# Opening a fused attention and retention layer: the first projection group as a written-out pipeline over the tiles of x

## The chip, the cores and the metric

The kernel runs on one core of one Trainium2 chip. The metric is the device time of one launch in microseconds. Of the kernel before, three timed runs and one profiled execution are at hand. The engines are named as in the profile: PE (TensorE; PEld are its weight loads), ACT (ScalarE), DVE (VectorE), POOL (GpSimd) and SP, which issues the DMAs. SPq is SP's queue.

## The reference

One layer of a streaming encoder works on 2048 prompt rows and 64 sample rows of width 1024. Only its beginning matters here:

```python
def layer_inputs(x, norm_g, w_in, b_gate, qn_g, kn_g):
    h = rmsnorm(x, norm_g) @ w_in
    qa, ka, va, za, qb, kb, vb, zb, ga, gb = jnp.split(h, _split_points(), axis=-1)
    ...

def rmsnorm(x, g=None):
    xf = x.astype(jnp.float32)
    y = xf * lax.rsqrt(jnp.mean(xf * xf, axis=-1, keepdims=True) + EPS)
    if g is not None:
        y = y * g.astype(jnp.float32)
    return y.astype(x.dtype)
```

The rest of the layer is differential attention (prompt rows among themselves, sample rows against a cache of 4096 keys), a retention branch, two gated output projections, a last projection and the residual. The first group of columns computed is va, the 512 columns of the attention's values, which are also an output.

## The kernel before, in words

**Precision.** The big products are made from two parts. A float32 operand a is split into a high part (`h`, a cast) and a low part (`l`, the rest), and a product is the sum of three matmuls: high by high, high by low, low by high. x is kept normalised, transposed and split as `xh` and `xl`; a piece of W (128 rows by 512 columns in the groups that matter here) as `wh` and `wl`.

**Tiles and groups.** x is worked on in two halves of 1024 rows. The first has nine tiles: eight of 128 prompt rows and one of the 64 sample rows. A group is 512 (wide) or 256 columns of W applied to all tiles of the half. The first three groups of the first half are wide: va, then ka, then qa. A tile of a wide group is eight chunks of the inner dimension, three matmuls each, 24 matmuls of 512 columns, into one of two PSUM buffers `mm`.

**From x to xh and xl.** `x_prep` (L250) issues the load of a tile and spawns `x_norm` (L303), which puts on ACT the square with its row sum (L308), a logarithm and an exponential (L310, L311); on DVE the mean (L315), a Newton step for the inverse root (L318 to L320), and the scaling of the tile by the root and the norm row (L327, two halves of 512 in the first half of x). `x_tile` (L331) transposes the scaled tile on PE in two lots of four (L341, into the single PSUM buffers `tp` and `pv`), casts each lot to `xh` on ACT (L348) and subtracts to `xl` on DVE (L349).

**The norm row.** In the first half `norm_g` is loaded as one row into `gz` and spread to 128 partitions by a matmul of one row of a constant matrix `ones` with it (`spread`, L285, L290); the sum stays in the two PSUM buffers `s` and is read by L327. Ten calls of `warm` follow (L297), each a matmul of `ones` by itself that nobody reads. Six such calls stand ahead of everything (L1667).

**W.** `w_load` (L365) issues the pieces of W into staging buffers, the first eight at once, the rest when more than four tiles of x are ready. `w_split` (L405) casts each piece on ACT (L415) and subtracts on POOL (L422), two of the first eight on DVE (L419).

**The first tile.** `mm_first` (L459) does the 16 matmuls with `wh` first (L470) and then the 8 with `wl` (L475); the other tiles go through `mm_group` (L442, L451). After a tile, `fin_va` copies the sums twice on ACT (L600, L602), subtracts on DVE (L604) and stores three times; its buffer `thi` exists once.

**What sets the order.** The program is a set of generators (tasks) run by `loop` (L82) with a planner's clock: `self.pe` is the planned time of PE, and A, V, G and ld advance planned times of ACT, DVE, POOL and the DMAs. A task yields a time or a condition and is resumed when the planned time is reached; among tasks that are ready the smallest priority number goes first. So the order of instructions on PE, ACT and DVE, the three engines named in `MANUAL` (L1676), is the order in which the tasks happen to put them; these engines then work strictly by semaphores. `x_prep`, `w_load` and `w_split` have priority 0, `x_norm` 1, `x_tiles` 2, and the stream of groups (`w_stream`, L1552, calling `natural`, L478) 9. POOL and SP are not in `MANUAL`; their instructions are placed by the framework. Loads are gated by `XFLY` (three tiles of x in flight in the first half) and by the count of W pieces issued: x tile 1 may go after four pieces, tile 2 after eight (L262).

Of the kernel before, what the change touches and what calls it, by code (L numbers as in the profile page):

```python
# [8 lines left out]
F32 = mybir.dt.float32  # L9
# [3 lines left out]
ALU = mybir.AluOpType  # L13
# [3 lines left out]
T = 2048  # L17
NS = 64
TT = T + NS
D = 1024  # L20
KC = 8
PAST = 4096
EPS = 1e-6
# [13 lines left out]
LAT = 250.0  # L37
# [6 lines left out]
STAGE = ["ws", "ws", "ws", "ath", "ath", "atl", "atl", "ev"]  # L44

# [11 lines left out]
class Hybrid:  # L57
# [192 lines left out]
    def x_prep(self, half):  # L250
        nc = self.nc
        self.xq = []
        self.xfly = 0
        yield from self.take("row", 2)
        gn = self.row("gn") if half else None
        jk = self.row("xjk")
        if half == 0:
            self.give("row", 0.0)
        tiles = self.xtiles(half)
        left = [len(tiles)]  # L260
        for j, (src, r, seg, col) in enumerate(tiles):
            yield lambda: self.xfly < XFLY[half] and (half > 0 or self.wloads >= min(4 * j, 8))  # L262
            self.xfly += 1
            yield from self.take("row")
            xt = self.row("xt")[:r]
            self.xq.append(None)
            tx = self.ld(xt, src, 4096 * r)
            if j == 0 and half == 0:
                yield from self.take("row")
                gz = self.row("gz")  # L270
# [3 lines left out]
                tg = t + 1200  # L274
                self.spawn(self.spread(gn, gz, t), 10)
# [9 lines left out]
    def spread(self, gn, gz, t):  # L285

        yield t
        for k in range(2):
            yield from self.take("s")
            self.nc.tensor.matmul(gn[k], self.ones[0:1, :], gz[0:1, 512 * k:512 * k + 512], start=True, stop=True)  # L290
# [12 lines left out]
    def x_norm(self, j, xt, jk, gn, t, tg, r, seg, col, left):  # L303
        nc = self.nc
        yield t
# [3 lines left out]
        t = self.A(1024, self.pe, 190)  # L309
# [3 lines left out]
        t2 = self.A(1, 0, 40)  # L313
        yield t
        nc.vector.tensor_scalar(ms, ss, 1.0 / D, EPS, op0=ALU.mult, op1=ALU.add)  # L315
        self.V(1, t)
        yield t2
        nc.vector.tensor_scalar(ms, y, y, ms, op0=ALU.mult, op1=ALU.mult)  # L318
        nc.vector.tensor_scalar(ms, ms, -0.5, 1.5, op0=ALU.mult, op1=ALU.add)
        nc.vector.tensor_scalar(y, y, ms, 128.0 if isinstance(gn, list) else 1.0, op0=ALU.mult, op1=ALU.mult)  # L320
        for _ in range(3):
            t = self.V(20, t2)
        if tg > self.pe:
            yield tg
        for k, g in enumerate(gn if isinstance(gn, list) else [gn]):
            sl = slice(512 * k, 512 * k + g.shape[1])
            nc.vector.scalar_tensor_tensor(out=xt[:, sl], in0=xt[:, sl], scalar=y, in1=g[:r], op0=ALU.mult, op1=ALU.mult)  # L327
        self.xq[j] = (xt, self.V(1100, t), r, seg, col)
        left[0] -= 1

    def x_tile(self, j):  # L331
# [3 lines left out]
        yield t  # L335
# [69 lines left out]
    def w_split(self):  # L405
        nc = self.nc
        nw = n = 0
        for c0, wide in self.order[0] + self.order[1]:
            for q in range(8 if wide else 4):
                yield lambda: len(self.wst) > 0  # L410
                st, t, tag = self.wst.pop(0)
                (h, l), tags = yield from self.w_room(wide, nw, q)
                if t > self.pe:
                    yield t
                nc.scalar.copy(h, st)  # L415
                th = t = self.A(512, self.pe)
                if n in (4, 6):
                    yield t
                    nc.vector.tensor_sub(l, st, h.bitcast(F32))  # L419
                    t = self.V(512, t)  # L420
                else:
                    nc.gpsimd.tensor_sub(l, st, h.bitcast(F32))  # L422
                    t = self.G(512, t)
                self.give(tag, t)
                if wide:
                    self.wq.append((h, l, t, tags, th))
                else:
                    self.wq.append((h[:, 0], l[:, 0], t, (), th))
                    self.wq.append((h[:, 1], l[:, 1], t, tags, th))
                n += 1  # L430
            nw += wide
# [10 lines left out]
    def mm_group(self, ps, n, us, wsl, x, wfirst, last):  # L442
        nc = self.nc
        seg, xsl = x
        for c in range(KC):
# [10 lines left out]
            if c % 2 and c < KC - 1:  # L456
                yield self.pe

    def mm_first(self, ps, us, r):  # L459

        nc = self.nc
        xh, xl = self.xh[0], self.xl[0]
        for c in range(KC):
            if len(us) <= c:
                yield lambda: len(self.wq) > 0
                us.append(self.wq.pop(0))
            if us[c][4] > self.pe:
                yield us[c][4]
            for i, x in enumerate((xh, xl)):
                nc.tensor.matmul(ps, x[:, c, :r], us[c][0], start=c == 0 and i == 0, stop=False)  # L470
                self.P(512)
        for c in range(KC):
            if us[c][2] > self.pe:
                yield us[c][2]
            nc.tensor.matmul(ps, xh[:, c, :r], us[c][1], start=False, stop=c == KC - 1)  # L475
            self.P(512)

    def natural(self, half, fin, fresh=False, wide=False):  # L478
        us = []
        tiles = self.xtiles(half)  # L480
        per, n = (1, 512) if wide else (2, 256)
        for j0 in range(0, len(tiles), per):
# [3 lines left out]
            for u, (src, r, seg, col) in enumerate(group):  # L486
                if fresh:
                    yield lambda: len(self.xt_ready) > j0 + u
                    yield self.xt_ready[j0 + u]
                if fresh and j0 == 0 and wide:  # L490
                    yield from self.mm_first(ps, us, r)
                else:
                    yield from self.mm_group(ps[:r, n * u:n * u + n], n, us, slice(0, n),
                                             (seg, slice(col, col + r)), False, j0 + u == len(tiles) - 1)
                if u < len(group) - 1:
                    yield self.pe
# [1055 lines left out]
    def w_stream(self):  # L1552
# [28 lines left out]
        self.seg_free = [0.0, 0.0]  # L1581
        self.xh, self.xl = [None, None], [None, None]
        self.wst = []
# [4 lines left out]
        self.spawn(self.x_tiles(9), 2, "w")  # L1588
# [52 lines left out]
    def run(self):  # L1641
# [18 lines left out]
        with tc.manual_schedule(engines=MANUAL(ET)):  # L1660
# [6 lines left out]
            self.warm(6)  # L1667
# [73 lines left out]
```

## Time and profile before

| what | value |
|---|---|
| three timed runs | 2017.9, 2019.16, 2020.87 us; median 2019.16 |
| profiled execution, time | 2016.98 us |
| its span | 2015.2 us |
| mean granted clock of PE | 0.997 |
| PE busy | 1991.4 us, 99% of the span |
| ACT, DVE, POOL busy | 956.9, 992.8, 419.2 us |
| one 512-column matmul in the first group, start to start | 0.23 us |
| ACT's square of a tile of x (L308) | 1.06 us |
| ACT's cast of a piece of W (L415) | 0.62 us |
| POOL's subtraction of a piece of W (L422) | 1.27 to 1.74 us in the first 80 us |
| load of a tile of x, 512 KB, issue to landing | 3.5 to 8.3 us |

The profile is of one execution. A line of a timeline gives the start and the duration in us, the engine, the line of the kernel, the operation, the tile written and the tiles read, shapes and a count; in brackets stands the time that the engine was idle before it and what released it. Matmuls are pipelined, so durations of neighbours overlap, and the distance of starts is the better measure. A line of the table of stages gives, for a stretch of time, the busy time of PE, PEld, DVE, ACT and POOL with the number of instructions, then the granted clock of PE as a share of full speed, the share of time that the DMA engines were busy, and GB/s. Time to landing is from a DMA's issue to its end.

### The profile page before, as it was taken

What the parts mean: (1) busy time and instruction counts of PE and PEld (TensorE: products, weight loads), DVE (VectorE), ACT (ScalarE), POOL (GpSimd) and SP (SyncE); (2) the same over time, 40 slices, a digit from 0 to 9 for tenths busy, and PEclk for the clock granted to TensorE, in tenths of its full rate; (3) what the DMA queues carried; (4) which work ended last, traced back from release to release, by engine and by line L of the source; (5) the groups of instructions that cost most, each with busy time, mean ns of one, the idle gap of its engine ahead of it and who ended that gap; (6) DMA issues with size and microseconds to landing.
All of it is one profiled execution on the core that took longest, in us unless ns stands there. A gap on an engine that the chain in (4) does not pass through costs nothing. (4 is left out here: it accounts for less than half of the span.)

```text
span 2015.2 us, 34341 instructions
## 1 busy us (share of the span) xinstructions
PE 1991.4 (99%) x12414; PEld 1786.1 (89%) x12414; DVE 992.8 (49%) x2659; ACT 956.9 (47%) x2096; POOL 419.2 (21%) x387
## 2 busy tenths in 40 slices
PE   8999999999999999999999999999999989999999
PEld 6778999999998999999999888888888878889997
DVE  6353575553331321546856655635653365444442
ACT  6332676654432433535666665645654544333221
POOL 2310121121112221221211111222112443222210
PEclk9999999999999999999999999999999999999999
DMA  6646464344565463563352252463234665444431
GB/s 228 195 146 171 135 168 130 101 140 144 150 182 131 135 178 104 164 198 123 112 157 87 85 158 68 124 190 95 64 92 126 202 216 159 144 146 133 140 94 58
DMA packets 330268, 280.96 MB, mean 139 GB/s; under 512 B 64689, under 2 KB 296113, under 8 KB 330098
## 3 DMA queue, kind: packets, MB, share of 16 engines
q1 hardware_dynamic: 330098, 278.77, 46.8%
q8 instruction: 98, 1.61, 0.3%
q14 instruction: 72, 0.59, 0.1%
HBM read 187.19 MB, written 91.49 MB: 138 GB/s over the span
## 5 line engine op out<-in xcount | busy, mean ns | idle before, releaser
L451 PE MATMUL mm<-xh,wh 128*128 128x512 f32 (+2 forms) x1280 | 461.1, 360 | 0.0
L451 PE MATMUL mm<-xh,wl 128*128 128x512 f32 (+2 forms) x1280 | 451.7, 353 | 0.0
L451 PE MATMUL mm<-xl,wh 128*128 128x512 f32 (+2 forms) x1280 | 450.9, 352 | 0.0
L422 POOL TENSOR_TENSOR wl<-ws,wh 128x512 fp32r<-128x512 f32 x190 | 251.9, 1338 | 912.3 <-ACT wh L415 632.2
L451 PE MATMUL mm<-wh,xh 128*128 128x256 f32 (+3 forms) x864 | 272.5, 315 | 0.3 <-DVE tlo L604 0.3
L451 PEld LDWEIGHTS mm<-xh,wl 128*128 128x128 f32 x1280 | 240.9, 188 | 31.9
L451 PEld LDWEIGHTS mm<-xh,wh 128*128 128x128 f32 x1280 | 241.2, 188 | 29.6 <-issue 0.2
L451 PEld LDWEIGHTS mm<-xl,wh 128*128 128x128 f32 x1280 | 241.5, 189 | 29.1
L451 PE MATMUL mm<-wh,xl 128*128 128x256 f32 (+3 forms) x864 | 267.2, 309 | 0.0
L451 PE MATMUL mm<-wl,xh 128*128 128x256 f32 (+3 forms) x864 | 266.9, 309 | 0.0
L661 ACT COPY ev<-mm 128x512 f32<-128x512 f32 x140 | 71.6, 511 | 238.8 <-PE mm L451 216.9
L451 PEld LDWEIGHTS mm<-wh,xh 128*128 128x128 f32 (+1 forms) x864 | 162.5, 188 | 11.0 <-PE s L836 0.4
L451 PEld LDWEIGHTS mm<-wl,xh 128*128 128x128 f32 (+1 forms) x864 | 162.7, 188 | 10.6
L451 PEld LDWEIGHTS mm<-wh,xl 128*128 128x128 f32 (+1 forms) x864 | 162.5, 188 | 10.2
L957 DVE TENSOR_TENSOR atl<-at,ath 128x512 fp32r<-128x512 f32 (+1 forms) x144 | 93.8, 660 | 139.8 <-ACT ath L955 139.8
L874 ACT ACTIVATE row<-row,a_mx 128x1024 f32<-128x1024 f32 (+7 forms) x160 | 153.6, 964 | 16.7 <-DVE a_mx L854 16.6
L844 DVE CUSTOM_DVE_ANT_0 row<-s,dfar 128x512 f32<-128x512 f32 (+2 forms) x192 | 117.9, 632 | 74.7 <-PE s L836 73.5
L415 ACT CAST wh<-ws 128x512 fp32r<-128x512 f32 x192 | 117.0, 619 | 40.7 <-PE mm L451 28.3
L955 ACT CAST ath<-at 128x512 fp32r<-128x512 f32 (+1 forms) x144 | 79.6, 563 | 99.3 <-PE at L942 96.9
L835 PE MATMUL s<-K,q 128*128 128x512 f32 (+3 forms) x320 | 120.3, 381 | 2.5 <-DVE a_acc L844 2.5
L836 PE MATMUL s<-K,q 128*128 128x512 f32 (+3 forms) x320 | 115.5, 362 | 0.7 <-DMA q<-qT 0.7
L895 DVE SCALAR_TENSOR_TENSOR row<-row,a_w 128x1024 f32<-128x1024 f32 (+4 forms) x96 | 98.1, 1032 | 26.7 <-ACT row L892 26.5
(206 smaller groups left out, 3945.5 us busy)
## 6 DMA issues: line engine op xcount, KB each, us to landing
ws<-in_w_in_dram SPq DMA_DIRECT2D x192, 256.0 KB, 3.1
q<-qT SPq DMA_DIRECT2D x128, 128.0 KB, 3.0
V<-vN SPq DMA_DIRECT2D x24, 512.0 KB, 5.5
K<-kT SPq DMA_DIRECT2D x48, 256.0 KB, 4.4
gt<-gaT SPq DMA_DIRECT2D x64, 132.0 KB, 2.1
gt<-gbT SPq DMA_DIRECT2D x64, 132.0 KB, 2.2
xt<-in_x_prompt_dram SPq DMA_DIRECT2D x16, 512.0 KB, 6.3
kn<-in_cache_k_T_dram SPq DMA_DIRECT2D x32, 256.0 KB, 3.9
```

The source lines that it names most:

```text
L415: nc.scalar.copy(h, st)
L422: nc.gpsimd.tensor_sub(l, st, h.bitcast(F32))
L451: nc.tensor.matmul(ps, p, q, start=c == 0 and i == 0, stop=c == KC - 1 and i == 2)
L661: nc.scalar.copy(ev, ps)
L835: nc.tensor.matmul(ps, q1s, kk, start=True, stop=False)
L836: nc.tensor.matmul(ps, q2s, kk, start=False, stop=True)
L844: nc.vector.tensor_tensor_reduce(out=units[k0 // 1024][:, k0 % 1024:k0 % 1024 + n], in0=ps, in1=tab, scale=-SLOPES[h], scalar=3.0e38, op0= ...
L874: nc.scalar.activation(u, u, AF.Exp, bias=mx, scale=-1.0, accum_out=lp[:, k:k + 1])
L895: nc.vector.scalar_tensor_tensor(out=u0, in0=u0, scalar=w[:, 0:1], in1=u1, op0=ALU.mult, op1=ALU.add)
L955: nc.scalar.copy(ah[:, :w], at[:, :w])
L957: nc.vector.tensor_sub(al[:, :w], at[:, :w], ah[:, :w].bitcast(F32))
```

## The change

The first group no longer goes through `natural` and four tasks; a new function `opening` writes the order of all its work out. `mm_first` and the task `x_tiles` for the first half are gone; `x_norm` is cut into four functions (`norm_sums` on ACT, `norm_mean`, `norm_root` and `norm_scale` on DVE) that `opening` calls one by one; `w_split` is cut into `w_piece` (cast on ACT) and `w_low` (subtraction), and waits until the opening is over. `between`, called by `mm_group` after the second and the fourth chunk of a tile, puts the sums of tile j+2 and then the transposes of tile j+1 and the scaling of tile j+2 into tile j. In tile 0 the order of the 24 matmuls is a list: H is `xh` by `wh`, X is `xl` by `wh`, L is `xh` by `wl`, T1 the transposes of tile 1.

x tile 1 is loaded ahead of all of W. Of the first eight pieces of W, three are subtracted on DVE (the fifth, seventh and eighth) instead of two. The norm row is put in a `gz` of 128 rows, of which the others are zeroed by a memset on DVE and one on POOL, and is spread by matmuls over all 128 rows; its load comes after that of `ident` instead of before. Ten warm calls stand ahead in place of six, and five after the spread in place of ten.

The core of the diff:

```diff
+OPENING = [(k[0], int(k[1])) for k in ("H0 X0 H1 X1 H2 X2 L0 H3 X3 L1 H4 X4 L2 T1 H5 X5 L3 H6 X6 L4 "
+                                       "H7 X7 L5 L6 L7").split()]
...
     def x_prep(self, half):
...
-            yield lambda: self.xfly < XFLY[half] and (half > 0 or self.wloads >= min(4 * j, 8))
+            yield lambda: self.xfly < XFLY[half] and (half > 0 or j < 2 or self.wloads >= 8)
...
-                t = self.ld(gz[0:1, :], self.i["norm_g"][0:1, :], 4096)
+                self.nc.vector.memset(gz[:, :512], 0.0)
+                self.nc.gpsimd.memset(gz[:, 512:], 0.0)
                 self.ld(self.ident, self.i["c_ident"], 1 << 16)
+                tg = self.ld(gz[0:1, :], self.i["norm_g"][0:1, :], 4096)
...
-            self.spawn(self.x_norm(j, xt, jk, gn, tx, tg, r, seg, col, left), 1, "w")
+            self.xin.append([xt, jk, gn, tx, tg, r, seg, col, left])
+            if half:
+                self.spawn(self.x_norm(j), 1, "w")
...
-            self.nc.tensor.matmul(gn[k], self.ones[0:1, :], gz[0:1, 512 * k:512 * k + 512], start=True, stop=True)
+            self.nc.tensor.matmul(ps, self.ones, gz[:, 512 * k:512 * k + 512], start=True, stop=True)
             t = self.P(2048)
         self.give("row", t)
-        for _ in range(10):
-            yield self.pe
-            self.warm(1)
+        self.warm(5)
...
-                if n in (4, 6):
-                    yield t
-                    nc.vector.tensor_sub(l, st, h.bitcast(F32))
...
+    def w_low(self, wide, n, st, h, l, t, tag, tags):
+        th = t
+        if n in (5, 7, 8):
+            self.nc.vector.tensor_sub(l, st, h.bitcast(F32))
...
             if c % 2 and c < KC - 1:
                 yield self.pe
+                if between:
+                    yield from between(c)
+
+    def opening(self, fin):
...
+        yield lambda: len(self.xin) > 0
+        self.norm_sums(0)
+        self.norm_mean(0)
+        self.norm_root(0)
+        yield from self.spread()
+        self.norm_scale(0)
+        yield lambda: len(self.xin) > 1
+        self.norm_sums(1)
+        for _ in range(2):
+            yield from (yield from self.w_piece(False))
+        self.norm_mean(1)
+        self.norm_root(1)
+        yield from self.x_tile(0, False)
+        self.norm_scale(1)
+        for _ in range(6):
+            low.append((yield from self.w_piece(False)))
+        for g in low[:4]:
+            yield from g
...
+        for k, c in OPENING:
+            if k == "T":
+                yield from self.x_tile(1, False)
+                self.norm_sums(2)
+                for g in low[4:]:
+                    yield from g
...
+                self.norm_mean(2)
+                self.norm_root(2)
+                continue
...
+            nc.tensor.matmul(ps, x, w, start=(k, c) == ("H", 0), stop=(k, c) == ("L", KC - 1))
...
+        self.spawn(fin(ps, 128, 1, 0, self.pe + LAT), 0, "w")
+        self.norm_scale(2)
+        self.opened = True
+        for j in range(1, 9):
+            def between(c):
+                if c == 1 and j + 2 < 9:
+                    yield lambda: len(self.xin) > j + 2
+                    self.norm_sums(j + 2)
+                if c == 3 and j + 1 < 9:
+                    if j + 2 < 9:
+                        self.norm_mean(j + 2)
+                        self.norm_root(j + 2)
+                    yield from self.x_tile(j + 1, False)
+                    if j + 2 < 9:
+                        self.norm_scale(j + 2)
...
+            yield from self.mm_group(ps[:r], 512, us, slice(0, 512), (seg, slice(col, col + r)), False,
+                                     j == 8, between)
...
     def natural(self, half, fin, fresh=False, wide=False):
+        if fresh and wide:
+            yield from self.opening(fin)
+            return
...
-            self.warm(6)
+            self.warm(10)
```

More of the change, by code (lines that the diff above doesn't have):

```diff
@@ L250, in x_prep @@
     def x_prep(self, half):
-        nc = self.nc
         self.xq = []
+        self.xin = []
         self.xfly = 0
[L254 to L258, printed above, removed]
+        gn = jk = tg = None
+        if half:
+            yield from self.take("row", 2)
+            gn, jk = self.row("gn"), self.row("xjk")
+        else:
+            yield from self.take("row")
+            jk = self.row("xjk")
         tiles = self.xtiles(half)
```

163 lines of the change are left out of this document (98 added, 65 removed).

## The prediction

> **What bounds the kernel now.** I read the page first: engine shares and the chain that ended last.
>
> ```profile
> span 2015.2 us, 34341 instructions
> PE 1991.4 (99%) x12414; PEld 1786.1 (89%) x12414; DVE 992.8 (49%) x2659; ACT 956.9 (47%) x2096; POOL 419.2 (21%) x387
> ```
>
> PE is the bound almost everywhere, so the change can only earn what PE loses in the first group. Then the timeline of PE over the first 80 us, to see where it loses time; columns are start, duration, instruction, and in brackets the idle time before it and its releaser.
>
> ```profile
> 1.05 2.93 PE L300 MATMUL at<-ones 128*128 128x128 f32 x12 [1.05 <-DVE epst L1666]
> 4.21 3.78 PE L290 MATMUL s<-gz,ones 1*128 1x512 f32 x4 [0.23 <-DMA gz<-in_norm_g_dram]
> 7.92 4.51 PE L300 MATMUL at<-ones 128*128 128x128 f32 x20
> 12.27 0.60 PE L341 MATMUL tp<-ident,xt 128*128 128x128 f32 x4
> ...
> 13.54 0.49 PE L470 MATMUL mm<-wh,xh 128*128 128x512 f32 x1 [0.24 <-ACT xh L348]
> ...
> 20.97 0.39 PE L451 MATMUL mm<-wh,xh 128*128 128x512 f32 x1
> ...
> 31.36 0.66 PE L341 MATMUL tp<-ident,xt 128*128 128x128 f32 x4 [3.86 <-DVE xl L349]
> ```
>
> The first useful matmul starts at 13.54, tile 1 at 20.97 (the first L451), and PE stands 3.86 us before 31.36. The same view puts the first matmul of the next group at 76.93. Third, the timeline of DVE says why PE stood: the two xl subtractions of x tile 2 start only at 30.63 and 31.23, because the norm scaling of a later tile was queued ahead of them.
>
> ```profile
> 27.77 0.69 DVE L604 TENSOR_TENSOR tlo<-mm,thi 128x512 fp32r<-128x512 f32 x1 [0.23 <-ACT raw L602]
> ...
> 29.30 1.41 DVE L327 SCALAR_TENSOR_TENSOR xt<-xt,x_st,s 128x512 f32<-128x512 f32 x2
> ...
> 30.63 0.68 DVE L349 TENSOR_TENSOR xl<-tp,xh 128x512 fp32r<-128x512 f32 x1
> ```
>
> Fourth, the table of stages (last three columns: granted clock, DMA share, GB/s) shows what the stand cost afterwards.
>
> ```profile
> 31.00:32.00 1.00, 0.64 (x5) 0.46 (x5) 0.91 (x2) 0.00 (x0) 0.00 (x0) 1.00 0.98 351
> 32.00:33.00 1.00, 1.00 (x7) 0.93 (x7) 0.32 (x1) 0.94 (x2) 0.00 (x0) 0.82 0.17 31
> 33.00:34.00 1.00, 1.00 (x4) 0.71 (x3) 0.37 (x1) 0.97 (x3) 0.00 (x0) 0.50 0.15 37
> ```
>
> The clock fell to 0.50 and came back at 36.0; matmuls start 0.43 us apart there and 0.2285 us elsewhere.
>
> **What the stage would be without loss.** A tile is 24 matmuls x 0.2285 = 5.48 us. Its eight transposes add 0.88 (46.84 to 47.63, plus 0.09 on the slower first matmul); the 64-row sample's add 0.7. Tiles 1 to 8 hold 192 matmuls (43.87), the transposes of tiles 2 to 7 (5.28) and of the sample (0.7): 49.85 us. They took 76.93 - 20.97 = 55.96, so 6.1 us are lost: 4.0 of standing, the rest at the half clock.
>
> **The change, part by part.**
>
> *Warm matmuls and spread.* Ten calls in place of six make 20 records; 20 take 4.32 us at 7.92, so they run from 1.05 to 5.4. The grant column says 1.00 here, but these records are 0.216 us apart at 128 columns, so I take the clock to be half; the four transposes of 12.27 (0.43 to the next four, against 0.60 at 31.36) are the first fast ones. The spread keeps its four records. At the old spacing (0.865) they end at 8.9, at a full clock (0.43) at 7.1. The row gz now waits for two memsets. That on VectorE: 128 columns take 0.165 and one takes 0.06, so 512 take some 0.5 and end at 1.6. That on GpSimd is not in the trace: above 0.10 (its 128x1 memset), below 1.27 (its 128x512 subtraction, which does more); I take 0.7, in between. So gz is issued at 1.6 to 2.2 instead of 1.20, and by the old 3.0 us is there at 4.6 to 5.2, still under the warm matmuls: nothing on PE. But x1 and all of W queue behind it on SP, up to 0.6 us; I charge 0.3. Scaled x0 is ready at 8.4 to 9.9 (VectorE is free at 6.85; two scalings of 0.75, the second after the spread), the five warm calls behind the spread end at 8.0 (fast) to 11.2 (slow), so x0 is transposed between 8.4 and 11.2, not 12.13.
>
> [...] The row: full-height matmuls from 7.92 to 12.2 came before the first fast record; one-row ones from 4.21 to 7.9 brought no fast one. [...]
>
> *x1 ahead of W.* Landings in before, as issue plus time to landing: x0 4.2, w0 6.2, w1 8.0, w2 8.8, w3 9.3, x1 10.7, w4 11.3, w7 13.3, x2 14.5. x1 (512 KB) takes the place of w0 and w1, so it lands near 8.0 + 0.3; w0 and w1 near 9.1 and 9.6; w2 to w7 after that up to 13.6, x2 as before. On ACT the new order is: square and root of x1, then casts of w0 and w1, then xh of x0. From a square's start to the cast behind it takes 1.63 (13.86 to 15.49), casts are 0.55 apart: square 8.3, w0 9.93, w1 10.48, xh 11.0, first matmul 11.65 (xh to matmul 0.64, as 12.90 to 13.54). That is **1.9 us earlier**; x0's transposes are hidden. Bounds: x1 at 6.2 (w0's place) gives 9.9, x1 at 10.7 (its own old place) gives 14.0: -3.6 to +0.5.
>
> *Tile 0, written out.* Counted from its first matmul. X0 follows at 0.73 as before. W casts follow the two xh at 1.1, 1.65, 2.2, 2.7, 3.3, 3.85, ahead of H2 to H7. GpSimd subtracts w0 and w1 before and w2, w3, w5 until 5.4 (1.3 each): L0 to L3 and L5 don't wait. The transposes of x1 come at 3.5 (scaled at 2.8). VectorE: two xl until 1.3, scaling of x1 until 2.8, w4's part until 4.1, x1's xl until 6.0, then w6 and w7 at 0.85 each (the smaller of the two such rows, 0.85 and 1.77, GpSimd being idle then): 6.9 and 7.75. So L6 and L7 wait, and the tile ends at 8.05; without a wait it would be 6.4. Before it took 20.97 - 13.54 = 7.43: **0.6 us lost**. Bounds: both parts at 0.69 (the cheapest 512-column subtraction) give 7.7, both at 1.77 give 9.9.
>
> *Tiles 1 to 8.* Per tile of 6.36 us, ACT has two copies, two xh, square and roots: 1.2 + 1.1 + 1.65 = 3.95; VectorE 0.69 + 1.4 + 0.9 + 1.41 = 4.4. In the new order the xl of tile j+1 stand ahead of the scaling of tile j+2. From the tile's start: copies until 1.35, square and roots until 3.1, transposes at 2.75, xl ready at 5.4, needed at 6.36; scaling ends at 6.8, needed at 9.1. The stand of 3.86 goes, and with it the fall of the clock. What is late next is the xl, with 1.0 us to spare, then the W casts of the next group in ACT's queue. I keep 0.5 us of loss: 50.35 against 55.96, **5.6 us saved**. Bounds: 6.1 saved, or with 0.5 us of loss in each of eight tiles 2.1.
>
> *Next group's W.* Its first three pieces, loaded now only at tile 3's end, are cast near 40 to 45, as now (45.06); all eight were split by 61.3 and are needed from 70 on. No cost.
>
> *Sum:* -1.9 + 0.6 - 5.6 = -6.9 us; the group ends at 70.0. What follows is PE-bound and starts earlier as a whole. The profiled execution took 2016.98 (2015.2 of span, 1.78 around it): 2010.1. The median of the runs shown, 2019.16, is 2.2 above it; on that footing **2012.3**. The bounds add up to -9.7 and +0.3.
>
> **Rivals.**
>
> 1. *The clock falls again.* After the warm calls PE has only transposes until 11.65. [...] What the rows show: with PE empty from 27.4 to 31.36 the clock fell at 32.4 and was back 3.7 us later, at a cost of some 2.2 us. Here the gap is 0.5 to 3.6 us (from 11.2 or 8.0 to 11.65), shorter. Price +2.2: 2014.5. Chance 0.15.
> 2. *The order on SP isn't the written one.* Only PE, ACT and DVE are ordered by hand; in before, table loads that the program emits after this group were issued at 32.9. If x1 lands late and w8 onwards or the constants are pulled into the x loads, xh waits per tile: the upper bounds of the first and third step, 0.5 + 0.6 - 2.1 = -1.0: 2018.2. Chance 0.15.
> 3. *Slower: ACT blocked by a store.* There is one thi buffer, and the trace has ACT's L600 waiting 2.30 us at 55.52 for the store vN<-thi. Stores stand on SP behind W loads that wait for GpSimd (up to 4.2 us, 11.6 in all). ACT has 2.4 us of slack per tile (6.36 - 3.95); a wait of 4.2 in every tile makes PE stand 1.8 in each of eight: 14.4, against the 6.9 of the sum, so 7.5 slower than before: 2026.7. It turns into a loss once PE stands more than 0.86 us per tile (6.9 / 8). Against it: the rows from 36 to 77 show the same waits and no stand of PE. Chance 0.08.
>
> **How the numbers follow.** Forecast 0.62, alone within 2009.5 to 2015. Rivals 0.15, 0.15, 0.08. The range takes in the lower bound and the first two rivals: 2008 to 2018.5; it leaves out the third rival and the tails. A measurement of this kernel can tell about 0.2%, 4 us: faster is below 2015.1 and holds the forecast and most of rival 1: 0.74. Same holds rival 2 and the rest: 0.18. Slower 0.08.
>
> **What would show it.** First matmul near 11.65 and behind ACT's xh, not behind the transposes; a wait of L6 and L7 on VectorE; no PE idle above 1 us between tile 1 and the group's end; granted clock 1.00 from 12 us on; next group's first matmul near 70.0. A first matmul after 13, a grant of 0.50, or PE waiting for xl or scaling in each tile would make it wrong; so would a later stage that gives the 7 us back.

## The result and the profile after

The changed kernel takes 2009.74 us (median of six runs, 2009.27 to 2012.72) against 2018.11 us for the kernel before in six runs beside them (2016.61 to 2020.87): a ratio of 0.9962 with an interval of 0.9952 to 0.9972, so about **8 us (0.4%) faster**. The profiled execution took 2009.56 us with a span of 2007.8 us, 7.4 us less span than before. The page opens like this:

```profile
span 2007.8 us, 34354 instructions
...
PE 1988.0 (99%) x12412; PEld 1784.0 (89%) x12412; DVE 991.3 (49%) x2661; ACT 955.6 (48%) x2096; POOL 420.3 (21%) x387
```

PE still bounds the kernel, with 3.4 us less of busy time and 4.0 us less of anything else (the span's 7.4). Where they went is read from the timeline of PE (start, duration, instruction, idle before and releaser):

```profile
1.05 4.64 PE L312 MATMUL at<-ones 128*128 128x128 f32 x20 [1.05 <-DVE epst L1768]
5.48 2.23 PE L300 MATMUL s<-gz,ones 128*128 128x512 f32 x4
7.55 1.28 PE L312 MATMUL at<-ones 128*128 128x128 f32 x10
8.66 0.60 PE L376 MATMUL tp<-ident,xt 128*128 128x128 f32 x4
...
10.48 0.49 PE L547 MATMUL mm<-wh,xh 128*128 128x512 f32 x1 [0.78 <-ACT xh L383]
...
16.79 1.58 PE L547 MATMUL mm<-wl,xh 128*128 128x512 f32 x3
18.21 0.40 PE L493 MATMUL mm<-wh,xh 128*128 128x512 f32 x1
```

The spread (L300) runs right behind the warm calls, the ten records behind it are already fast (0.11 us apart), and the first useful matmul stands at 10.48 instead of 13.54, behind ACT's xh. The last row but one covers L5, L6 and L7: three matmuls start to start in 1.42 us where 0.69 would do, the forecast wait of tile 0. Tile 1 begins at 18.21. The stand before tile 2 is gone. In DVE's timeline both xl subtractions of x tile 2 now stand ahead of the scaling of x tile 3; whether that order is the reason is tested below (scale_first, late_transposes).

```profile
22.23 0.69 DVE L384 TENSOR_TENSOR xl<-tp,xh 128x512 fp32r<-128x512 f32 x1 [0.39 <-ACT xh L383]
22.84 0.68 DVE L384 TENSOR_TENSOR xl<-pv,xh 128x512 fp32r<-128x512 f32 x1
23.44 1.40 DVE L347 SCALAR_TENSOR_TENSOR xt<-xt,x_st,s 128x512 f32<-128x512 f32 x2
```

The xl are ready at 23.5, 1.1 us before tile 2 starts at 24.61. The table of stages (PE busy first; last three columns granted clock, DMA share, GB/s) shows full clock from 10 us on:

```profile
10.00:18.00 8.00, 7.11 (x32) 5.20 (x33) 5.94 (x11) 6.65 (x14) 6.23 (x5) 1.00 1.04 410
18.00:30.00 12.00, 12.00 (x61) 10.04 (x62) 8.82 (x22) 7.39 (x16) 0.00 (x0) 1.00 0.76 218
30.00:50.00 20.00, 19.84 (x99) 15.92 (x98) 11.45 (x27) 12.82 (x28) 3.80 (x3) 1.00 0.56 197
```

In tiles 1 to 8 one loss stands out, and it has two causes in a row. ACT stood 5.29 us before the copy `thi` of tile 3:

```profile
34.86 0.59 ACT L383 CAST xh<-pv 128x512 fp32r<-128x512 f32 x1
40.74 0.59 ACT L698 CAST thi<-mm 128x512 fp32r<-128x512 f32 x1 [5.29 <-PE tp L376]
```

The releaser named is a transpose, but PE had ended tile 3 soon after 37.4, and what the copy writes is the single buffer `thi`, whose readers are DVE's subtraction (over at 33.3) and the store of tile 2. (In a second profile of the same kernel, change_again below, the same row names the store: 5.29 us before 41.35.) SP's timeline has that store behind three loads that the framework placed there:

```profile
31.40 0.43 SPq L136 DMA_DIRECT2D dfar<-in_c_dfar_dram  x1
31.88 0.43 SPq L136 DMA_DIRECT2D dnear<-in_c_dnear_dram  x1
32.35 1.09 SPq L136 DMA_DIRECT2D state<-in_state_ret_dram  x1
33.55 1.33 SPq L136 DMA_DIRECT2D vN<-thi  x1
```

The copy started 7.2 us after the store was issued. Everything behind it on ACT came late, the xh of the next tile last, and PE lost 0.7 us at 43.5 to 45.2:

```profile
43.53 0.40 PE L493 MATMUL mm<-wh,xl 128*128 128x512 f32 x1
43.96 0.50 PE L493 MATMUL mm<-wh,xh 128*128 128x512 f32 x1
44.30 0.40 PE L493 MATMUL mm<-wl,xh 128*128 128x512 f32 x1
44.83 0.50 PE L493 MATMUL mm<-wh,xl 128*128 128x512 f32 x1
```

The next group starts at 69.18 (before 76.93), and from there to the end of the span it is 1938.6 us against 1938.3: what the first group gains is carried through. The same remainder lies between 1937.0 and 1940.5 in all profiles below but one (start_thi2, whose buffers differ), so single executions differ by some 3 us behind the group whatever the edit. At the group's end the same kernel gave 69.18 and 70.03 in two profiles, so differences below 1 us between single executions show nothing there by themselves.

### The profile page after: what moved, and what is told of

It reads as the page before. It is cut to its first block, busy times and chain, and to the rows that moved or that the text cites. A ratio compares the mean times of both kernels' runs of the same rounds, so it can differ in the third digit from the quotient of the medians.

```text
span 2007.8 us, 34354 instructions
## 1 busy us (share of the span) xinstructions
PE 1988.0 (99%) x12412; PEld 1784.0 (89%) x12412; DVE 991.3 (49%) x2661; ACT 955.6 (48%) x2096; POOL 420.3 (21%) x387
## 5 line engine op out<-in xcount | busy, mean ns | idle before, releaser
L493 PEld LDWEIGHTS mm<-wh,xh 128*128 128x128 f32 (+1 forms) x864 | 162.2, 188 | 11.4 <-ACT xh L383 0.5
```

The lines of the kernel that those rows point to most:

```text
L493: nc.tensor.matmul(ps, p, q, start=c == 0 and i == 0, stop=c == KC - 1 and i == 2)
```

## The experiments

The table gives one profiled execution each (us); tile 0 counts from its first matmul to tile 1's. The ratio is to the kernel before, run beside it.

| kernel | first matmul | tile 0 | tiles 1 to 8 | next group | median | ratio and interval |
|---|---|---|---|---|---|---|
| before | 13.54 | 7.43 | 55.96 | 76.93 | 2018.11 | 1 |
| after | 10.48 | 7.73 | 50.97 | 69.18 | 2009.74 | 0.9962 [0.9952, 0.9972] |
| change_again | 10.32 | 7.73 | 51.98 | 70.03 | 2010.17 | 0.9966 [0.9953, 0.9978] |
| one_row_spread | 10.27 | 7.83 | 50.74 | 68.84 | 2010.71 | 0.9966 [0.9955, 0.9978] |
| no_warm | 10.82 | 7.73 | 51.93 | 70.48 | 2011.44 | 0.9971 [0.9962, 0.9981] |
| w_before_x1 | 13.05 | 9.71 | 50.24 | 73.00 | 2013.33 | 0.9981 [0.9972, 0.9991] |
| late_transposes | 9.71 | 7.73 | 56.48 | 73.92 | 2015.31 | 0.9992 [0.9983, 1.0001] |
| scale_first | 10.72 | 9.10 | 51.47 | 71.29 | 2011.91 | 0.9975 [0.9966, 0.9984] |
| before_full_spread | 9.73 | 7.41 | 57.76 | 74.90 | 2016.87 | 0.9999 [0.9989, 1.0008] |
| before_x1_first | 15.66 | 6.12 | 56.69 | 78.47 | 2017.17 | 1.0000 [0.9991, 1.0009] |
| start_thi2 | 10.83 | 7.40 | 56.34 | 74.57 | 2021.73 | one run |
| tuned | 10.74 | 8.54 | 50.13 | 69.41 | 2010.08 | 0.9965 [0.9954, 0.9976] |
| gap_filled | 10.44 | 7.31 | 50.14 | 67.89 | 2010.29 | 0.9959 [0.9946, 0.9971] |
| best_try | 10.83 | 7.51 | 50.23 | 68.57 | 2009.60 | 0.9955 [0.9942, 0.9969] |

**Theory.** The cover that the written-out order gives in tiles 1 to 8 brings some 5 us, x1 ahead of W some 3 us of an earlier start, and the height of the spread brings nothing. The rivals: the spread brings the start by waking the clock; the order of DVE alone brings the tiles' part; the start alone brings most of it.

**one_row_spread.** The changed kernel with the old one-row spread.

```diff
-                nc.vector.memset(gz[:, :512], 0.0)
-                nc.gpsimd.memset(gz[:, 512:], 0.0)
...
-            self.nc.tensor.matmul(ps, self.ones, gz[:, 512 * k:512 * k + 512], start=True, stop=True)
+            self.nc.tensor.matmul(ps, self.ones[0:1, :], gz[0:1, 512 * k:512 * k + 512], start=True, stop=True)
```

> The changed kernel with the norm row spread by one row again (no memsets), the ten warm calls ahead and five behind kept. Theory (the start hangs on x tile 1's landing and then on ACT's queue; ten warm calls are enough to release PE's clock near 6 us): first useful matmul stays near 10.5, the group ends near 69.2, time within 1 us of the changed kernel (2009.7). Rival (one-row matmuls don't count as activity, so the full-height spread is what releases the clock): spread from 5.4 to 8.9 at half clock, scaling to 9.7, warm calls to 11.1, first matmul 12.4, and if tile 0 still runs at half clock up to 4.8 us more: 2011.6 to 2016.5.

The time is that of the change (0.9966), and the first matmul came at 10.27. Yet the height does something. The table of stages:

```profile
7.00:8.00 1.00, 1.00 (x9) 1.00 (x9) 0.97 (x2) 0.94 (x5) 0.00 (x0) 0.90 1.03 295
8.00:9.00 1.00, 1.00 (x7) 1.00 (x7) 0.86 (x4) 0.93 (x3) 0.33 (x1) 0.50 1.00 344
...
11.00:12.00 1.00, 1.00 (x5) 0.87 (x5) 0.90 (x2) 1.00 (x3) 0.51 (x2) 0.89 1.06 412
```

The one-row matmuls ran fast (0.48 us apart from 5.06, against 0.93 in before), with nothing but the warm calls ahead of them; but PE was busy without a gap from 5 to 9, and the granted clock still fell, at 7.8 (a mean of 0.90 between 1.00 and 0.50), and came back at 11.2. In the two profiles of the change (after, change_again) its column says 1.00 there. The fall hit only the transposes and the first matmuls, which wait for ACT anyway. So the rival is right in so far as the clock did not stay up in the one profile with one-row matmuls, and wrong that it takes the full-height spread to bring full speed: here full speed was there behind the ten warm calls alone, as the theory says, which is right on the time as well.

**no_warm.** The changed kernel without the warm calls (one of the ten is left).

```diff
-        self.warm(5)
...
-            self.warm(10)
+            self.warm(1)
```

> The changed kernel with one warm call ahead and none behind the spread. Theory (the warm calls are worth the clock only, the start hangs on x1 and ACT): spread from 5.0 to 8.5 at half clock, x0 scaled at 9.3, first matmul 10.6; the clock isn't released by then, tile 0 runs at half rate for some 3.5 us: the group ends near 72.4, 2013. Rival (the calls are not needed): 69.2 and 2009.7.

```profile
4.34 3.75 PE L300 MATMUL s<-gz,ones 128*128 128x512 f32 x4 [2.50 <-DMA gz<-in_norm_g_dram]
7.89 1.06 PE L375 MATMUL tp<-ident,xt 128*128 128x128 f32 x4
8.94 1.12 PE L375 MATMUL pv<-ident,xt 128*128 128x128 f32 x4
10.82 0.51 PE L546 MATMUL mm<-wh,xh 128*128 128x512 f32 x1 [0.77 <-ACT xh L382]
```

The spread runs at half speed (its records are 0.89 us apart, the last two in the change 0.43) and ends near 8, and so do the transposes behind it (a row of four takes 1.06 us, against 0.60 in the change). The useful matmuls find full speed: from 11.88 on they are 0.23 us apart, and tile 0 takes 7.73 as in the change. The expected loss at half clock is not there, and the rival is right. The medians differ by 1.7 us (2011.44 against 2009.74), but the intervals overlap, so the warm calls are not shown to be worth anything here.

**w_before_x1.** The changed kernel with x tile 1 loaded behind four pieces of W, as before.

```diff
-            yield lambda: self.xfly < XFLY[half] and (half > 0 or j < 2 or self.wloads >= 8)
+            yield lambda: self.xfly < XFLY[half] and (half > 0 or self.wloads >= min(4 * j, 8))
```

> The changed kernel with x tile 1 loaded behind four pieces of W again, its order on the engines unchanged. Theory (ACT does x1's sums ahead of the first W casts, so x1's landing sets the start): x1 lands at 10.7 instead of 7.2, first matmul 14.0 instead of 10.48, the rest shifted: 2013.2. Rival (the start is set by the clock and the spread): first matmul below 11, 2010.

ACT's timeline, then PE's:

```profile
9.78 1.06 ACT L321 ACTIVATE xjk<-xt 128x1024 f32<-128x1024 f32 x1 [3.77 <-DMA xt<-in_x_prompt_dram]
```

```profile
13.05 0.80 PE L547 MATMUL mm<-wh,xh 128*128 128x512 f32 x1 [4.07 <-ACT xh L383]
```

The square of x1 stands ahead of the casts of W on ACT, so a late x1 holds the first matmul. PE was empty from 9.0 to 13.05, the clock fell (to 0.50 from 11.26 to 18.08, by the means of the stages), and tile 0 took 9.71 us instead of 7.73; the theory had no such fall in it. The time (2013.33) is what it gave (2013.2), in part by luck: the first matmul came 0.95 us before the expected 14.0, and the fall took 2.0 back. And tiles 1 to 8 keep their gain, 50.24, though tile 1 starts at 22.76, later than the 20.97 of before. So their gain does not come from the early start.

**late_transposes.** The changed kernel with the next tile's transposes and scaling behind a tile's matmuls, not after its fourth chunk.

```diff
-                    yield from self.x_tile(j + 1, False)
-                    if j + 2 < 9:
-                        self.norm_scale(j + 2)
...
             self.spawn(fin(ps[:r], r, 1, 128 * j if j < 8 else T, self.pe + LAT), 0, "w")
             yield self.pe
+            if j + 1 < 9:
+                yield from self.x_tile(j + 1, False)
+            if j + 2 < 9:
+                self.norm_scale(j + 2)
```

> The changed kernel with the transposes of tile j+1 (and the scaling of tile j+2) put behind the matmuls of tile j instead of into their middle, for tiles 1 to 8. Theory (the gain in tiles 1 to 8 is that copying and splitting xT is covered by matmuls): PE waits about 1.3 us per tile for the chain transposes, copies of the tile before, xh, xl: 7 tiles, some 9 us, clock not falling: 2019. Rival (the gain is the order on DVE, xl ahead of the next scaling, which is kept here): at most 0.3 per tile, 2012.

The view of waits from 18 to 75 us, for PE's weight loads (total, times, longest):

```profile
PEld mm L493 <- ACT xh L383: 4.6, 7, 1.9
PEld mm L493 <- DVE xl L384: 2.9, 7, 0.5
```

Seven tiles, seven waits for each: tile 1 takes 8.15 us and the next five 7.15 to 7.25, instead of 6.38. Tiles 1 to 8 took 56.48, more than before, and most of the gain was gone (0.9992). The cause stands; the size lies between theory and rival, at 0.8 us in most tiles.

**scale_first.** The changed kernel with the scaling of tile j+2 ahead of the transposes of tile j+1, so ahead of its xl on DVE.

```diff
-                    yield from self.x_tile(j + 1, False)
                     if j + 2 < 9:
                         self.norm_scale(j + 2)
+                    yield from self.x_tile(j + 1, False)
```

> The changed kernel with the scaling of tile j+2 put ahead of the xl of tile j+1 on DVE in tiles 1 to 7. Theory (matmuls cover it): xl is ready 1.4 us later, at 6.8 from the tile's start, when the first matmul that reads it is due at 6.8: at most 0.2 us per tile, 2009.7 to 2011.3. Rival (the order on DVE is what made PE stand before): 1.4 us or more per tile, 10 us: 2020.

Tiles 1 to 8 took 51.47, between the 50.97 and 51.98 of the two profiles of the change. One tile took 7.71 us instead of 6.38, with a stall of 1.05 us for xl at 47.0, behind a late copy `thi` (ACT had waited 4.40 us for the store); the others took no longer than in the change. DVE's order, by which the prediction explained the stand, is not what carries the gain: with the transposes laid under the tile, there is time for either order unless ACT is late. The rest of what this profile lost, it lost at the start, where the clock fell:

```profile
10.72 0.55 PE L547 MATMUL mm<-wh,xh 128*128 128x512 f32 x1 [1.76 <-ACT xh L383]
```

```profile
11.00:12.00 1.00, 0.82 (x2) 0.50 (x2) 1.00 (x3) 1.00 (x3) 1.00 (x2) 0.51 1.09 410
12.00:13.00 1.00, 1.00 (x4) 0.77 (x3) 1.00 (x2) 1.00 (x3) 1.00 (x2) 0.50 1.00 410
...
14.00:15.00 1.00, 1.00 (x5) 0.77 (x5) 0.05 (x1) 0.27 (x1) 1.00 (x1) 0.78 1.01 406
```

That is the prediction's first rival. Nothing in the edit acts before 10.72 on PE: in this execution the warm calls ended early (7.7) and x1 landed late (7.45), so PE had eight transposes and then nothing for 1.8 us. Tile 0 took 9.10, 1.4 us more than 7.73.

**before_full_spread.** The kernel before with the new start alone (memsets, full spread, warm calls 10 and 5).

```diff
+                nc.vector.memset(gz[:, :512], 0.0)
+                nc.gpsimd.memset(gz[:, 512:], 0.0)
-                t = self.ld(gz[0:1, :], self.i["norm_g"][0:1, :], 4096)
                 self.ld(self.ident, self.i["c_ident"], 1 << 16)
+                t = self.ld(gz[0:1, :], self.i["norm_g"][0:1, :], 4096)
...
-            self.nc.tensor.matmul(gn[k], self.ones[0:1, :], gz[0:1, 512 * k:512 * k + 512], start=True, stop=True)
+            self.nc.tensor.matmul(gn[k], self.ones, gz[:, 512 * k:512 * k + 512], start=True, stop=True)
...
-        for _ in range(10):
+        for _ in range(5):
...
-            self.warm(6)
+            self.warm(10)
```

> The kernel before with only the first part of the change: gz zeroed by memsets and loaded after ident, spread by all 128 rows, ten warm calls ahead and five behind. x1 still comes after four pieces of W, and the order of the tiles is the old one. Theory (parts of the start and of the tiles add up): the clock is released near 6, x0 is transposed near 8.7, ACT's first four W casts end near 10, first matmul 10.6 instead of 13.54; the stand in tile 2 and the fall of the clock stay: the group ends near 74.0, 2.9 us faster than before (2014.9). Rival (what comes first in the start is taken back later in the group, because landings or ACT set the stand): the group ends at 76.9, no gain (2017.8).

The first matmul came 3.8 us earlier, tile 1 too (17.14). At the group's end of this profile 2.0 us of it are left (74.90 against 76.93, between theory and rival), in the time nothing that can be told from the spread (0.9999, with 2 us to either side). Here the stand before tile 2 grew from 3.86 to 6.00 us. In the order SP, ACT, PE:

```profile
17.95 0.33 SPq L132 DMA_DIRECT2D vN<-thi  x1
```

```profile
24.98 0.59 ACT L602 CAST thi<-mm 128x512 fp32r<-128x512 f32 x1 [3.34 <-DMA vN<-thi]
```

```profile
29.68 1.11 PE L343 MATMUL tp<-ident,xt 128*128 128x128 f32 x4 [6.00 <-DVE xl L351]
```

Tile 0 ends earlier, so its store goes out earlier, into the loads of x (362 GB/s from 18 to 24), and is over only 7.0 us later. ACT holds back the copy `thi` of tile 1 until then, with the xh of x2 behind it; DVE's scaling and xl follow, then PE. The rival that the old order gives the head start back is right for about half of it.

**start_thi2.** That kernel with two `thi` buffers (and, for the room, one `ev` less, so that its total is not comparable).

```diff
-BUFS = {"thi": 1, "tlo": 2, "ev": 3, "q": 2, "K": 4, "V": 4, "ath": 2, "atl": 2,
+BUFS = {"thi": 2, "tlo": 2, "ev": 2, "q": 2, "K": 4, "V": 4, "ath": 2, "atl": 2,
```

> The kernel before with the new start (as in the run before_full_spread) and two buffers thi instead of one, paid for by two ev instead of three. Only the first group is looked at, since the ev buffers are used all over. Theory (what took the head start back is ACT standing 3.3 us at thi for tile 0's store, which lands at 25 whatever the start): no wait of thi for a store at tile 1, xl of tile 2 some 2.5 us earlier, tile 2 starts near 28.8 instead of 31.3 and the group ends near 72.4. Rival (the landings of the later x tiles set the stand): tile 2 starts at 31, the group ends at 74.9 as without the second buffer.

ACT, then PE:

```profile
23.92 0.59 ACT L602 CAST thi<-mm 128x512 fp32r<-128x512 f32 x1 [1.21 <-PE mm L453]
```

```profile
28.62 0.66 PE L343 MATMUL tp<-ident,xt 128*128 128x128 f32 x4 [3.86 <-DVE xl L351]
```

The copy now waits for its own matmuls, the stand is back at 3.86, and tile 1 takes 11.5 us (18.23 to 29.75) instead of 14.2. The store was what enlarged it. The group's end (74.57) is only 0.3 us earlier, not at the expected 72.4: this execution started 1.1 us later, and tile 2 took 8.0, not 7.1, since it ran at half speed from 29.75 to 32.9 (products 0.43 us apart; in before_full_spread from 31.3 to 32.7).

**before_x1_first.** The kernel before with x1 ahead of W alone.

```diff
-            yield lambda: self.xfly < XFLY[half] and (half > 0 or self.wloads >= min(4 * j, 8))
+            yield lambda: self.xfly < XFLY[half] and (half > 0 or j < 2 or self.wloads >= 8)
```

> The kernel before with only x tile 1 loaded ahead of W. Theory (in the old start the warm calls at half clock hold PE until 12.27, so x1's place does nothing there): first matmul stays at 13.5, the group ends within 1 us of 76.9, 2017.8. Rival (the load order alone moves the start): first matmul near 11 to 12, 2 us faster.

No gain (1.0000). The theory has the time right, not the start: the planner now puts the transposes of x1 (14.51) ahead of tile 0, whose first matmul waits until 15.66, and the group ends at 78.47. The early load helps only in the order that was written for it.

**tuned.** The changed kernel with the second W cast behind x0's xh on ACT, and DVE's last two low parts of W ahead of x1's xl.

```diff
-        for _ in range(2):
-            yield from (yield from self.w_piece(False))
+        yield from (yield from self.w_piece(False))
...
-        for _ in range(6):
+        for _ in range(7):
...
-        for g in low[:4]:
+        for g in low[:5]:
...
+                for g in low[5:]:
+                    yield from g
                 yield from self.x_tile(1, False)
                 self.norm_sums(2)
-                for g in low[4:]:
-                    yield from g
```

> The changed kernel with two places of its order altered: the second W cast behind the two xh of x0 on ACT (so only one cast stands between x1's sums and xh), and the low parts of the last two W pieces ahead of x1's xl on DVE. Theory (these two queues hold PE in tile 0): first matmul 0.5 earlier after x1's landing, the wait of L6 and L7 (0.9) gone: the group ends near 67.8, 2008.3. Rival (the waits move on, xl of x1 or the late W cast hold PE instead): 69.2, 2009.7.

Both expected gains came: the first matmul 2.75 us behind x1's landing instead of 3.28, and no wait at the end of tile 0 (from L5 to tile 1 it is 18.60 to 19.28, three times 0.23). But x1 landed at 7.99, the clock fell again (0.85 from 10 to 12, 0.50 from 12 to 14), tile 0 took 8.54, and no gain is left to measure (0.9965).

**gap_filled.** The changed kernel with four warm calls between the transposes of x0 and the first matmul.

```diff
         yield from self.x_tile(0, False)
+        self.warm(4)
         self.norm_scale(1)
```

> The changed kernel with four more warm calls between the transposes of x0 and the first matmul of tile 0. Theory (in some executions the clock falls there, because from the last warm call to the first matmul PE has only transposes and nothing): the granted clock stays 1.00 from 8 to 16 us and tile 0 takes 7.7 us whatever the landing of x1; first matmul at most 0.5 later when x1 lands early; time 0 to 1 us below the changed kernel's in the same runs. Rival (the clock there depends on something else): a granted clock of 0.50 still shows in tile 0, which then takes 8.5 to 9.1.

```profile
9.19 0.60 PE L376 MATMUL pv<-ident,xt 128*128 128x128 f32 x4
9.63 1.06 PE L312 MATMUL at<-ones 128*128 128x128 f32 x8
10.44 0.48 PE L548 MATMUL mm<-wh,xh 128*128 128x512 f32 x1
```

The granted clock stays at 1.00 to the group's end, which comes at 67.89, the earliest of all. The median (2010.29) does not differ from the change: in the profile of the change the clock did not fall either. Nor does this show that the four calls prevent a fall: x1 landed early here (6.49), and without them the stretch from the last warm call to the first product would have been at most 1.7 us, where the change has 1.8 and no fall.

**best_try.** The edits of tuned and gap_filled, and the loads of dfar and dnear held back by a memset of one column of each on DVE.

```diff
+        self.nc.vector.memset(self.dfar[:, 0:1], 0.0)
         self.ld(self.dfar, self.i["c_dfar"], 1 << 19)
...
+        self.nc.vector.memset(self.dnear[:, 0:1], 0.0)
         self.ld(self.dnear, self.i["c_dnear"], 1 << 18)
```

> The changed kernel with the two altered queues of the run tuned, the four warm calls of gap_filled, and the two attention tables loaded only after the group (a one-column memset on DVE holds each load back), so that the store that thi waits for at tile 3 doesn't queue behind them. Theory (three small losses add up: 0.9 of L6 and L7, 0.7 at tile 4, up to 1.4 of clock): first group 2 us shorter than in the changed kernel, 2007.7 against 2009.7. Rival (such losses are given back later or lie within the spread of the landings): within 0.7 us of the changed kernel.

```profile
37.80 0.59 ACT L698 CAST thi<-mm 128x512 fp32r<-128x512 f32 x1 [2.12 <-PE mm L493]
```

With those loads out of the way, the copy that stood until 40.74 goes right behind its matmuls, and PE has no stall from tile 1 to the group's end. In all other profiles with the changed kernel's tile order these loads stand ahead of that store or beside it, and ACT waits for the store at this tile: 3.0 us (gap_filled), 3.8 (tuned), 4.4 (scale_first), 4.7 (w_before_x1), 5.1 (one_row_spread), 5.3 (after, change_again), 5.4 (no_warm). Up to 4.7 PE loses at most 0.1 us to it in the order of the change, from 5.1 on 0.5 or more. So the store behind these loads is the cause of the 0.7 us. How late the copy starts after the end of its tile orders the cases better than the wait does: 2.5 us late cost PE nothing (gap_filled), 2.7 cost 0.1 (w_before_x1), 3.2 cost 0.6 (one_row_spread), 3.4 cost 0.7 (after), 3.6 cost 1.0 (no_warm), 4.1 cost 1.5 (change_again). The cover is worth some 2.6 us of lateness; what goes beyond it PE pays in full. The whole is 0.6 us less than the change run beside it, by medians (expected were 2); the intervals overlap, so it is not shown to be faster.

**change_again.** The changed kernel once more, unaltered, beside the two above.

> The changed kernel once more, unaltered, as the measure for the other runs of this call. Theory: x1 lands at 6.2 to 8.0 and the first matmul follows by 3.3; the group ends at 68.5 to 71, depending on that and on the clock in tile 0; time 2009.7 within 1 us. Rival (the first profile was a lucky one): group end above 71 and a time above 2011.5.

The change again takes 0.9966. This time ACT was late by more (PE waits 0.80 us at 44.56), and the group ends at 70.03: the same program varies by 0.9 us at that point.

## Why the prediction was right, point by point

*First matmul, forecast 11.65, came at 10.48.* The chain was the forecast one (x1, square, two casts of W, xh), and so were its steps: 7.20 to 8.82 for the square to the first cast (1.62, forecast 1.63), 0.65 from xh to the matmul. **The mis-sized term is the landing of x1**, 7.2 and not 8.3. It was taken from the landing of the second piece of W in before, plus 0.3 for the later queue; the runs show it to be no constant. Issued at 2.03 to 2.09 in nine profiles, it came at 6.24, 6.37, 6.49, 7.05, 7.20, 7.28, 7.45, 7.54 and 7.99. A landing should have entered as a range. w_before_x1 shows the dependence: 9.78, and the first matmul at 13.05.

*Tile 0, forecast 8.05, took 7.73.* L6 and L7 waited for DVE as worked out. The two subtractions took 1.28 together, not 1.70: the forecast used the row of 0.85, which shared its time with POOL, and with POOL idle they cost what a 512-column subtraction costs elsewhere (0.69). Where they ran beside POOL's own subtractions they took 0.85 and 1.77 us in before, and 0.86 for the one at 12.98 in the change.

*Tiles 1 to 8, forecast 50.35, took 50.97.* The stand and the fall of the clock went. The forecast named DVE's queue as what the change mends, and in before it did hold the stand: DVE was free for the xl at 28.4 and began them at 30.63, 2.2 of the 3.86 us. But it is not what the gain rests on: scale_first, with the old order on DVE, loses 1.3 us in one tile and nothing in the others, while late_transposes shows the time between the transposes and the first use of their xh and xl to be worth 4.5 to 5.5 us (56.48 against 51.98 and 50.97). The forecast's own sentence, xl ready 1.0 us ahead of need, gave that margin (1.1 in the trace) but put the credit on the queue. Of the 1.1 us lost against the 49.85 without loss, 0.7 are at one tile, by the mechanism of the third rival (a `thi` copy held by a store). It was priced for every tile at 4.2 us; it struck one, at 5.3 us, of which ACT's slack and the cover left 0.7 to PE.

*The clock (first rival).* It did not fall in either profile of the change, but it did in those of scale_first and tuned: of the five profiles with this start or nearly so (after, change_again, late_transposes, scale_first, tuned) two had a fall. A chance of 0.15 was low, and that the change's own profile was spared is luck. Counting from the last warm call to the first product of tile 0: 3.0 us (scale_first), 2.9 (tuned) and 5.2 (w_before_x1) had a fall; 1.8 (after), 1.5 (change_again) and 1.3 (late_transposes) had none. The means of the stages put the falls at 11.0, 11.4 and 11.3, which is 3.3, 3.5 and 3.4 us after the last warm call, though PE held transposes for the first 1.0 to 1.3 us of that. The price was 1.0 us (tuned's tile 0, 8.54, against best_try's 7.51) to 1.4, and 2.0 in w_before_x1, where the half clock lasted twice as long; the forecast had 2.2. The prediction's reading of before is slightly off: the row of 0.82 puts the fall near 32.65, and the clock was back 3.4 us later, not 3.7.

*How long a fall lasts, and what decides it.* By the means of the stages the granted clock was at 0.50 for 3.4 us in before (32.65 to 36.06), scale_first (11.02 to 14.44), tuned (11.40 to 14.82) and one_row_spread (7.80 to 11.22), and for 6.8 us in w_before_x1 (11.26 to 18.08) and before_full_spread (25.84 to 32.64). What decides a fall is not shown. The stretch without products was near 3 us or more where it fell behind the warm calls, but in one_row_spread it fell with PE busy from 1.05 on, in before 1.3 us after PE had begun again (31.36), and no_warm has 2.9 us without products (7.9 to 10.82, the first 2.2 of them transposes) under a column of 1.00; there the spread ahead of that stretch and the transposes in it ran at half speed, so its 1.00 says little.

*The other rivals.* At the start SP's order was the written one (x1 at 2.09, W from 2.49), and the stores of the other tiles cost PE nothing. The table loads that the second rival names did come into the group, from 31.40 on: they delayed a store, not an x tile.

*The sum.* 10.48 + 7.73 + 50.97 = 69.18 against 70.05: three errors of -1.2, -0.3 and +0.6, which cancel in part. The profiled time came out 0.5 us below the 2010.1 forecast on that footing, the median 2.6 below 2012.3. The 2.2 us added to pass from profile to median were an accident of three runs: six runs put the median of before at 2018.11, 1.1 above its profile, and the median of after is 0.2 above its own. The bounds are added up wrongly in the prediction: by its own terms (-3.6 to +0.5, 7.7 to 9.9 against 7.43, 6.1 to 2.1 saved) they come to -9.4 and +0.9, not -9.7 and +0.3; the range stands without it.

*The parts are not additive.* The new start alone gives 0.9999, x1 alone 1.0000, both new start and new order with x1 late 0.9981, all of it 0.9962 (each within 0.001, or 2 us). The forecast summed three terms and was right because it took them together; for the start alone the sum of parts promised 2.9 us, which the time does not show, and for x1 alone the forecast's term of 1.9 us would not have come either.

*Open.* Why one load lands 1.8 us earlier or later is not settled. No run tests warm calls in the gap in an execution whose clock would have fallen without them.

## What to carry to other kernels

An earlier start is worth its time only if the stage behind it can take it in: follow the first result to its store and to the buffer that the store frees, before counting the gain. Work that feeds the next tile belongs in the middle of the present one (here worth 4.5 to 5.5 us in the group), with a margin larger than one delayed DMA; the order within that margin matters only where something has used the margin up. A landing time read from one profile is one sample: carry its spread (here 6.24 to 7.99) through the sum.

## What the runs showed of the hardware

- A 256 KB store issued into a stream of loads (362 GB/s from 18 to 24) was over only 7.0 us later (17.95 to 24.98, before_full_spread); the median store of this kind takes 3.0 us in the profile of the change. Here that delay, not the store's size, decided what one buffer cost.
- A fall of the granted clock to 0.50 lasted 3.4 us in four profiles (before, scale_first, tuned, one_row_spread) and 6.8 us in two (w_before_x1, before_full_spread), by the means of the stages. Products were 0.43 us apart in it, and 0.2285 at 1.00.
- In one_row_spread the granted clock fell from 1.00 to 0.50 at 7.8 while PE ran the one-row matmuls and the warm calls behind them without a gap from 5.06. In the two profiles of the change, with the spread over 128 rows, it stayed at 1.00.
- In the first microseconds of a trace the column of the granted clock says 1.00 although matmuls run at half speed: in after 20 records of 128 columns take 4.43 us from 1.05 on, 0.22 each, and ten from 7.55 on 0.11 each; in before they are 0.216 us apart from 7.92 to 12.2, in no_warm four transposes take 1.06 us at 7.89 and 1.12 at 8.94. The starts of the instructions have to be read there.
- A 512-column subtraction of W on DVE took 0.68 us with POOL idle (after, 16.53) and 0.85 and 1.77 us beside POOL's (before, from 17.69), and POOL's 1.74 at 17.95 instead of 1.29 at 16.70.
- Memsets of 128 x 512 float32 took 0.48 us on DVE and 0.53 on POOL; 0.5 and 0.7 were estimated.
